# One split instead of two for the weight factors of products 5 and 6 in an output projection

## The chip, the cores and the metric

The kernel runs on one core of one Trainium2 chip. Times are device microseconds (us) of one execution; the time of a kernel is the median of its runs. Engines: PE is TensorE, PEld its weight loads, DVE is VectorE, ACT is ScalarE, POOL is GpSimd, SP is SyncE, which issues the DMAs of the weights.

## The reference

One encoder layer on x of 512 tokens by 1024 channels, all in float32: a feed-forward network, a mixer and a second feed-forward network, each with a norm before and after and a residual.

```python
def swiglu(x, w_in, w_out):
    gate, up = jnp.split(x @ w_in, 2, axis=-1)     # w_in  1024 x 5632
    return (jax.nn.silu(gate) * up) @ w_out        # w_out 2816 x 1024
...
y_mix = mixer(...)      # gated convolution on half of the channels, chunked mLSTM on the other half
```

The change touches only the product with `w_out`, which is done once in each of the two feed-forward networks (FFN).

## The kernel before

**Split numbers.** Each float32 operand of a matmul is split into a high part, rounded to the type that PE multiplies, and a low part, the rest. `split(hi, lo, src)` is two instructions: an ACT copy into `hi` (L273, CAST in the trace) and a DVE subtraction `lo = src - hi` (L274). A product takes three matmuls: hi x hi, hi x lo, lo x hi. So each weight costs a cast on ACT and a subtraction on DVE before PE can use both of its parts.

**The FFN.** The hidden size of 2816 is 22 columns `h` of 128 (`hcol(k)`). The in-projection makes each of them by a scheme of seven products (matmuls at L400, 12 in each product; helpers on DVE L464 to L470 and L448, on ACT L456 to L467). The last column's products are not needed until late in the out-projection, and the scheduler may put them between the out-projection's matmuls.

**The out-projection.** 22 steps over k. The first ten are taken in pairs: a pair of h columns times the two weight rows that belong to it, by seven products instead of eight, with sums and differences of halves as factors. It is done in two passes, by a list `OUT`:

- five "a" steps (pairs 0 to 4): `w_out_a` builds the weight factors of products 1, 7, 5 and 6 from the raw rows r0 (128 x 1024) and the right half of r1 (three subtractions at L183, then splits); `left_a` the factors from h (L492 on DVE, splits into `big`). Matmuls at L525.
- then `taken(1)`, `taken(5)` and so on copy the sums out of PSUM (ACT L535 for product 1, L537 for product 5);
- then five "b" steps (products 2, 3 and 4, `w_out_b`) in turn with plain steps (L550), and the other plain steps.

In the first pass one more number is kept for the second one: the difference that is the sixth factor, `kept` (five tiles of 128 x 512), which `w_out_b` subtracts (L206).

**What sets the order.** The program is written without engine order: the tile scheduler simulates the program and fixes the order of instructions on each engine when it is built. Each engine then runs its queue in that order and waits at the head of it. A change of one instruction's size or engine can therefore move others. Buffers come from pools: 4 raw weight tiles (`rawp`), 12 split weights (`wpool`), 13 of h and its factors (`big`), 6 temporaries of 128 x 512 (`t2`), 2 of 128 x 1024 (`t4`), 8 PSUM banks.

Of the kernel before, what the change touches and what calls it, by code (L numbers as in the profile page):

```python
# [37 lines left out]
def encoder_kernel(ctx: ExitStack, tc: tile.TileContext, a: dict, out: bass.AP):  # L38
    nc = tc.nc
# [14 lines left out]
    def nm(s):  # L54
        uid[0] += 1
        return f"{s}_{uid[0]}"
# [7 lines left out]
    def t2(dt=F32):  # L64
        return t2p.tile([P, 512], dt, tag="t2", name=nm("t2"))
# [7 lines left out]
    def f32(ap):  # L73
        return ap.bitcast(F32)
# [101 lines left out]
    kept = []  # L176

    def w_out_a(r0, r1):

        c = (slice(0, 512), slice(512, 1024))  # L180

        def sub(o, a_, b_):
            nc.vector.tensor_tensor(out=o, in0=a_, in1=b_, op=ALU.subtract)  # L183

        def wt(n):
            return wpool.tile([P, 1024], F32R, tag="w", name=nm(n))

        sub(r1[:, c[0]], r0[:, c[1]], r0[:, c[0]])
        sub(r0[:, c[1]], r1[:, c[1]], r0[:, c[1]])
        t = t2()  # L190
        sub(t, r1[:, c[1]], r1[:, c[0]])
        kept.append(t)
        ah, al = wt("whi"), wt("wlo")
        split(ah, al, r0)
        bh, bl = wt("whi"), wt("wlo")
        split(bh[:, c[0]], bl[:, c[0]], r1[:, c[0]])
        split(bh[:, c[1]], bl[:, c[1]], t)
        return {1: (ah[:, c[0]], al[:, c[0]]), 7: (ah[:, c[1]], al[:, c[1]]),
                5: (bh[:, c[0]], bl[:, c[0]]), 6: (bh[:, c[1]], bl[:, c[1]])}

# [71 lines left out]
    def split(hi, lo, src, eng=nc.vector):  # L272
        nc.scalar.copy(out=hi, in_=src)  # L273
        eng.tensor_tensor(out=lo, in0=src, in1=f32(hi), op=ALU.subtract)  # L274
# [831 lines left out]
```

## Time and profile before

| what | value |
| --- | --- |
| median of 3 runs | 925.3 us (924.71 to 926.23) |
| the profiled execution | 924.99 us, of which the span is 923.3 us |
| granted PE clock | 0.998 |
| PE busy | 906.5 us, 6015 matmuls |
| DVE busy | 713.2 us, 1192 instructions |
| ACT busy | 446.4 us, 753 instructions |
| POOL busy | 42.3 us, 64 instructions |

The span is the profiled time from the first to the last instruction. In rows of a group, "x199 | 240.7, 1217" reads as 199 instructions, 240.7 us in all, 1217 ns each; what follows is the idle time ahead of them and what ended it. In a timeline a row begins with start and duration; equal instructions that follow each other are joined (x12), and brackets give idle time ahead of them and its releaser. In the first FFN the first pass stands at about 232 to 265 us of the span, in the second at about 792 to 825 us.

### The profile page before, as it was taken

What the parts mean: (1) busy time and instruction counts of PE and PEld (TensorE: products, weight loads), DVE (VectorE), ACT (ScalarE), POOL (GpSimd) and SP (SyncE); (2) the same over time, 40 slices, a digit from 0 to 9 for tenths busy, and PEclk for the clock granted to TensorE, in tenths of its full rate; (3) what the DMA queues carried; (4) which work ended last, traced back from release to release, by engine and by line L of the source; (5) the groups of instructions that cost most, each with busy time, mean ns of one, the idle gap of its engine ahead of it and who ended that gap; (6) DMA issues with size and microseconds to landing.
All of it is one profiled execution on the core that took longest, in us unless ns stands there. A gap on an engine that the chain in (4) does not pass through costs nothing.

```text
span 923.3 us, 15016 instructions
## 1 busy us (share of the span) xinstructions
PE 906.5 (98%) x6015; PEld 822.4 (89%) x6015; DVE 713.2 (77%) x1192; ACT 446.4 (48%) x753; POOL 42.3 (5%) x64
## 2 busy tenths in 40 slices
PE   7999999999999999999999999999999999999997
PEld 7999999999877888987888888999999999977885
DVE  5988988888988358496777736889888888999434
ACT  6645555555456226452424425645545544565311
POOL 3000000000012001000011000000000000000000
PEclk9999999999999999999999999999999999999999
DMA  8433434343344514231422501314343333343502
GB/s 246 146 92 92 138 105 125 92 117 95 100 136 139 180 46 115 61 100 46 117 90 69 160 23 30 104 51 137 92 129 101 109 104 97 106 149 100 172 4 88
DMA packets 126542, 96.99 MB, mean 105 GB/s; under 512 B 4212, under 2 KB 114824, under 8 KB 126472
## 3 DMA queue, kind: packets, MB, share of 16 engines
q1 hardware_dynamic: 126472, 96.03, 35.2%
q8 instruction: 47, 0.77, 0.3%
q14 instruction: 23, 0.19, 0.1%
HBM read 93.92 MB, written 2.10 MB: 104 GB/s over the span
## 4 chain that ended last, share of the span: by engine, by line
PE 89%; DVE 6%; ACT 1%; DMA 1%; issue 1%; SPq 0%; POOL 0%; DVEq 0%; POOLq 0%; ACTq 0%
PE ps L400 42%; PE ps L550 13%; PE ps L391 12%; PE ps L525 8%; PE ps L1063 5%; PE ps L421 4%; PE ps L913 2%; DVE big L274 2%; DVE wlo L274 2%; DVE big L492 1%; DMA raw<-in_w_ffn_in_dram 1%; PE ps L980 1%; PE ps L987 1%; PE ps L318 1%; ACT whi L273 0%
## 5 line engine op out<-in xcount | busy, mean ns | idle before, releaser
L274 DVE TENSOR_TENSOR wlo<-raw,whi 128x1024 fp32r<-128x1024 f32 x209 | 247.3, 1192 | 63.7 <-ACT whi L273 47.1
L273 ACT CAST whi<-raw 128x1024 fp32r<-128x1024 f32 x211 | 211.9, 1029 | 153.0 <-DVE raw L150 46.8
L400 PE MATMUL ps<-big,whi 128*128 128x256 f32 x1920 | 264.9, 280 | 0.0
L400 PEld LDWEIGHTS ps<-big,whi 128*128 128x128 f32 x1920 | 243.4, 188 | 0.9 <-ACT whi L273 0.2
L400 PE MATMUL ps<-big,wlo 128*128 128x256 f32 x960 | 150.9, 280 | 0.0
L400 PEld LDWEIGHTS ps<-big,wlo 128*128 128x128 f32 x960 | 129.2, 188 | 0.0
L550 PE MATMUL ps<-whi,big 128*128 128x512 f32 x384 | 122.3, 396 | 0.2 <-ACT whi L273 0.2
L550 PEld LDWEIGHTS ps<-whi,big 128*128 128x128 f32 x384 | 72.0, 188 | 17.7 <-ACT whi L273 0.7
L391 PE MATMUL ps<-big,whi 128*128 128x512 f32 (+1 forms) x384 | 79.8, 358 | 0.0
L525 PE MATMUL ps<-whi,big 128*128 128x512 f32 x240 | 76.1, 395 | 2.8 <-ACT big L273 2.6
L550 PE MATMUL ps<-wlo,big 128*128 128x512 f32 x192 | 75.6, 395 | 0.0
L391 PEld LDWEIGHTS ps<-big,whi 128*128 128x128 f32 x384 | 63.5, 188 | 10.8 <-issue 0.2
L400 PE MATMUL ps<-big,ws 128*128 128x256 f32 x480 | 65.3, 280 | 0.0
L400 PEld LDWEIGHTS ps<-big,ws 128*128 128x128 f32 x480 | 60.3, 188 | 0.0
L525 PEld LDWEIGHTS ps<-whi,big 128*128 128x128 f32 x240 | 44.7, 188 | 13.8 <-ACT big L273 3.5
L462 ACT COPY t<-ps 128x256 f32<-128x256 f32 x40 | 14.9, 372 | 71.4 <-PE ps L400 71.3
L273 ACT CAST big<-big 128x512 fp32r<-128x512 f32 (+2 forms) x68 | 36.1, 583 | 22.7 <-DVE big L492 11.2
L525 PE MATMUL ps<-wlo,big 128*128 128x512 f32 x120 | 44.8, 393 | 0.0
L550 PEld LDWEIGHTS ps<-wlo,big 128*128 128x128 f32 x192 | 36.1, 188 | 8.5
L391 PE MATMUL ps<-big,wlo 128*128 128x512 f32 (+1 forms) x192 | 41.1, 356 | 0.0
L274 DVE TENSOR_TENSOR big<-big,big 128x512 fp32r<-128x512 f32 (+2 forms) x68 | 40.7, 635 | 0.1
L391 PEld LDWEIGHTS ps<-big,wlo 128*128 128x128 f32 x192 | 32.1, 188 | 5.5
(207 smaller groups left out, 1149.6 us busy)
## 6 DMA issues: line engine op xcount, KB each, us to landing
raw<-in_w_ffn_in_dram SPq DMA_DIRECT2D x88, 512.0 KB, 4.8
raw<-in_w_ffn_out_dram SPq DMA_DIRECT2D x44, 512.0 KB, 4.3
raw<-in_w_mix_in_dram SPq DMA_DIRECT2D x24, 512.0 KB, 3.7
raw<-in_w_mix_out_dram SPq DMA_DIRECT2D x8, 512.0 KB, 3.4
raw<-in_w_ffn_out_dram SPq DMA_DIRECT2D x10, 256.0 KB, 4.2
out_dram<-x SPq DMA_DIRECT2D x8, 256.0 KB, 2.9
x<-in_x_dram SPq DMA_DIRECT2D x4, 256.0 KB, 4.5
x<-in_x_dram SPq DMA_DIRECT2D x2, 512.0 KB
```

Source lines behind the costliest of these rows:

```text
L273: nc.scalar.copy(out=hi, in_=src)
L274: eng.tensor_tensor(out=lo, in0=src, in1=f32(hi), op=ALU.subtract)
L318: nc.tensor.transpose(out=pt[:, blk(k)], in_=xs[:, blk(4 * b + k)], identity=ident)
L391: nc.tensor.matmul(o, ww[:, k, :], xk(xT, xx, k, sl), start=n == 0, stop=n == 3 * KD - 1)
L400: nc.tensor.matmul(o, ww[:, k, :], x[xx][:, k, :], start=first and n == 0, stop=n == 11, skip_group_check=True)
L421: nc.tensor.matmul(o, ww[:, k, :], xq_hl(xq, (k // 4, th))[xx][:, k % 4, :], start=n == 0, stop=n == 3 * KD - 1)
L462: nc.scalar.copy(a_[:, h1], x[:, h0])
L492: nc.vector.tensor_tensor(out=o, in0=a_, in1=b_, op=op)
L525: nc.tensor.matmul(acc[tb + t][half], left[n][x][:, blk(t)], right[n][y], start=first and x == y == 0, stop=last_ and x == 1, skip_group_c ...
L550: nc.tensor.matmul(acc[tb][half], hT[hh][:, blk(tb)], w[ww][:, blk(half, 512)], start=fresh and hh == ww == 0, stop=k == NF - 1 and hh == ...
L913: nc.tensor.matmul(pv_, xk(xT, xx, k, blk(tb)), ww[:, k % 2, :], start=n == 0, stop=n == 3 * KD - 1)
L1063: nc.tensor.matmul(acc[half], yy[yi][:, k % 4, blk(tb)], wmo[k][wi][:, blk(half, 512)], start=(n == 0 and yi == 0 and wi == 0), stop=(n == ...
```

## The change

`w_out_a` no longer makes the sixth factor in a tile of its own. The third subtraction writes in place into the right half of r1. The fifth and sixth factor then lie side by side in r1 and are split in one operation of 128 x 1024, instead of two of 128 x 512. An ACT copy of the right half into a `t2` tile keeps the number that `w_out_b` needs.

```diff
         sub(r1[:, c[0]], r0[:, c[1]], r0[:, c[0]])
         sub(r0[:, c[1]], r1[:, c[1]], r0[:, c[1]])
-        t = t2()
-        sub(t, r1[:, c[1]], r1[:, c[0]])
-        kept.append(t)
+        sub(r1[:, c[1]], r1[:, c[1]], r1[:, c[0]])
         ah, al = wt("whi"), wt("wlo")
         split(ah, al, r0)
         bh, bl = wt("whi"), wt("wlo")
-        split(bh[:, c[0]], bl[:, c[0]], r1[:, c[0]])
-        split(bh[:, c[1]], bl[:, c[1]], t)
+        split(bh, bl, r1)
+        t = t2()
+        nc.scalar.copy(t, r1[:, c[1]])
+        kept.append(t)
```

The scheduler's order changes in the two first passes and near them, on PE, DVE and ACT; on POOL and SP it stays. In the rows below a number behind a name tells one buffer's use from another's; it is counted differently in the two programs. `raw` is a loaded weight, `whi` and `wlo` its high and low part, `ps` a PSUM bank, `big` an h tile or the split factors made of it.

PE, start of the first pass in the second FFN, before: `whi_1234` and `whi_1236` are the weights of step 0 (products 1 and 7, and 5 and 6), `whi_1241` those of step 1; the L400 rows are the last hidden column.

```order
L525 MATMUL ps_1251_8663<-whi_1234_8523,big_1261_8673 128x512
L525 MATMUL ps_1252_8664<-whi_1234_8523,big_1261_8673 128x512
L400 MATMUL ps_1245_8551<-big_922_6103,whi_1221_8408 128x256 x8
L400 MATMUL ps_1245_8551<-big_922_6103,wlo_1222_8409 128x256 x4
L525 MATMUL ps_1253_8665<-whi_1236_8527,big_1261_8673 128x512
L525 MATMUL ps_1254_8666<-whi_1236_8527,big_1261_8673 128x512
L400 MATMUL ps_1246_8552<-big_870_5860,whi_1221_8408 128x256 x8
L400 MATMUL ps_1246_8552<-big_870_5860,wlo_1222_8409 128x256 x4
L400 MATMUL ps_1245_8551<-big_923_6106,whi_1223_8412 128x256 x8
L400 MATMUL ps_1245_8551<-big_923_6106,wlo_1224_8413 128x256 x4
L525 MATMUL ps_1251_8663<-whi_1241_8541,big_1263_8708 128x512
L525 MATMUL ps_1252_8664<-whi_1241_8541,big_1263_8708 128x512
```

Before, three products of the last hidden column stand ahead of the first matmul of step 1. After, `whi_1235` holds products 5 and 6 of step 0, `whi_1240` and `whi_1242` the weights of step 1:

```order
L525 MATMUL ps_1251_8656<-whi_1240_8534,big_1263_8701 128x512
L525 MATMUL ps_1252_8657<-whi_1240_8534,big_1263_8701 128x512
L525 MATMUL ps_1255_8660<-whi_1235_8521,big_1261_8666 128x512
L525 MATMUL ps_1253_8658<-whi_1242_8538,big_1263_8701 128x512
L525 MATMUL ps_1254_8659<-whi_1242_8538,big_1263_8701 128x512
L525 MATMUL ps_1255_8660<-whi_1242_8538,big_1263_8701 128x512
L525 MATMUL ps_1251_8656<-wlo_1241_8535,big_1263_8701 128x512
L525 MATMUL ps_1251_8656<-whi_1240_8534,big_1263_8701 128x512
L525 MATMUL ps_1252_8657<-wlo_1241_8535,big_1263_8701 128x512
L525 MATMUL ps_1252_8657<-whi_1240_8534,big_1263_8701 128x512
L400 MATMUL ps_1245_8544<-big_922_6098,whi_1221_8403 128x256 x8
L400 MATMUL ps_1245_8544<-big_922_6098,wlo_1222_8404 128x256 x4
```

The products of the last hidden column moved behind these ten matmuls, nine of which belong to step 1.

DVE, same place, before (`wlo_1222` and `wlo_1224` are weights of the last hidden column, `wlo_1235` and `wlo_1237` those of step 0, `raw_1239` of step 1):

```order
L464 TENSOR_TENSOR t2_1230_8421<-ps_1226_8417,t2_1228_8419 128x256
L183 TENSOR_TENSOR t2_1233_8521<-raw_1232_8517 128x512
L274 TENSOR_TENSOR wlo_1222_8409<-raw_1215_8392,whi_1221_8408 128x1024
L274 TENSOR_TENSOR wlo_1224_8413<-raw_1216_8394,whi_1223_8412 128x1024
L469 TENSOR_TENSOR t2_1229_8420<-ps_1225_8416,t2_1229_8420 128x256
L274 TENSOR_TENSOR wlo_1235_8524<-raw_1231_8515,whi_1234_8523 128x1024
L470 TENSOR_TENSOR big_890_5906<-t2_1229_8420,t2_1230_8421 128x256
L274 TENSOR_TENSOR wlo_1237_8528<-raw_1232_8517,whi_1236_8527 128x512
L274 TENSOR_TENSOR wlo_1237_8528<-t2_1233_8521,whi_1236_8527 128x512
L183 TENSOR_TENSOR raw_1239_8535<-raw_1238_8533 128x512
```

After (`wlo_1234` and `wlo_1236` are step 0's):

```order
L469 TENSOR_TENSOR t2_1229_8415<-ps_1225_8411,t2_1229_8415 128x256
L274 TENSOR_TENSOR wlo_1224_8408<-raw_1216_8389,whi_1223_8407 128x1024
L470 TENSOR_TENSOR big_890_5901<-t2_1229_8415,t2_1230_8416 128x256
L274 TENSOR_TENSOR wlo_1234_8518<-raw_1231_8510,whi_1233_8517 128x1024
L274 TENSOR_TENSOR big_1261_8666<-big_885_5896,big_1261_8666 128x256
L274 TENSOR_TENSOR big_1261_8666<-t4_1262_8667,big_1261_8666 128x256
L183 TENSOR_TENSOR raw_1239_8529<-raw_1238_8527 128x512
L274 TENSOR_TENSOR big_1263_8701<-big_885_5896,big_1263_8701 128x256
L274 TENSOR_TENSOR big_1263_8701<-t4_1264_8702,big_1263_8701 128x256
L492 TENSOR_TENSOR big_885_5896<-t4_1262_8667,big_885_5896 128x256
L448 TENSOR_TENSOR big_890_5901<-ps_1225_8411,t2_1230_8416 128x256
L274 TENSOR_TENSOR wlo_1236_8522<-raw_1232_8512,whi_1235_8521 128x1024
```

L469 moved ahead of a weight's low part, and step 0's second weight moved behind the left factors' low parts and L492, L448.

ACT, end of the a steps in the first FFN, before (`wt_450` and `whi_453` are weights of the next steps, `big_451` the next left factor):

```order
L535 COPY big_414_3035<-ps_406_3027 128x512
L535 COPY big_414_3035<-ps_407_3028 128x512
L537 COPY big_414_3035<-ps_408_3029 128x512
L537 COPY big_414_3035<-ps_409_3030 128x512
L273 CAST wt_450_3246<-raw_447_3242 128x512
L273 CAST whi_453_3294<-raw_452_3292 128x1024
L273 CAST big_451_3286<-big_28_229 128x512
```

After:

```order
L535 COPY big_414_3033<-ps_406_3025 128x512
L273 CAST wt_450_3241<-raw_447_3237 128x512
L273 CAST whi_453_3289<-raw_452_3287 128x1024
L535 COPY big_414_3033<-ps_407_3026 128x512
L537 COPY big_414_3033<-ps_408_3027 128x512
L273 CAST whi_456_3295<-raw_455_3293 128x1024
L537 COPY big_414_3033<-ps_409_3028 128x512
L273 CAST big_451_3281<-big_28_229 128x512
```

Three casts of weights moved between the four copies of the sums.

## The prediction

> **What bounds the kernel now.** I read the busy times first, then what TensorE (PE) waits for, then the busy times of single stretches, and last the timelines around the places where the order changes.
>
> ```profile
> span 923.3 us, 15016 instructions
> ...
> PE 906.5 (98%) x6015; PEld 822.4 (89%) x6015; DVE 713.2 (77%) x1192; ACT 446.4 (48%) x753; POOL 42.3 (5%) x64
> ```
>
> PE is busy in 98% of the span, so only 17 us of idle time exist, and most of them lie elsewhere (start, mixer, end). The waits of PE name those of the output projections' first passes (source line, who released it, total, count, mean, in us):
>
> ```profile
> PE ps L525 <- ACT big L273: 2.6, 2, 1.3
> ...
> PE ps L525 <- ACT wt L273: 0.9, 1, 0.9
> ```
>
> The timeline shows each of them as a gap between rows (start, duration, engine, line). Matmuls of 512 columns follow each other every 0.23 us, so what exceeds 0.23 between two starts is a stall.
>
> ```profile
> 264.66 1.08 PE L525 MATMUL ps<-whi,big 128*128 128x512 f32 x4
> 267.05 0.50 PE L525 MATMUL ps<-whi,big 128*128 128x512 f32 x1 [1.31 <-ACT big L273]
> ...
> 279.76 2.05 PE L525 MATMUL ps<-wt,big 128*128 128x512 f32 x6
> ...
> 809.82 0.39 PE L525 MATMUL ps<-whi,big 128*128 128x512 f32 x1
> 810.40 0.50 PE L525 MATMUL ps<-whi,big 128*128 128x512 f32 x1 [0.19 <-DVE big L448]
> ...
> 839.52 0.39 PE L525 MATMUL ps<-whi,big 128*128 128x512 f32 x1
> 840.81 0.73 PE L525 MATMUL ps<-wt,big 128*128 128x512 f32 x2 [0.90 <-ACT wt L273]
> 841.75 0.50 PE L550 MATMUL ps<-whi,big 128*128 128x512 f32 x1 [0.21 <-ACT whi L273]
> ```
>
> Four matmuls from 264.66 end their starts at 265.35; the next begins at 267.05, so 1.5 us are lost there, and the second wait of 1.3 us in the first list is its twin in the second FFN. The six from 279.76 should take 5 x 0.23 + 0.39 = 1.54 and took 2.05: a stall of some 0.3 inside, the rest being the slower restart. At 810.40 the loss is 0.58 - 0.23 = 0.35; at 840.81 it is 1.29 - 0.23 = 1.06, and up to 841.75 another 0.4. All that the two first passes could give back is therefore about 5 us.
>
> VectorE (DVE) has no such slack where the first pass starts (columns: window, its length, then sum and count for PE, PEld, DVE, ACT and POOL, clock, DMA share, GB/s):
>
> ```profile
> 792.00:800.00 8.00, 8.00 (x55) 7.34 (x54) 7.88 (x18) 4.12 (x9) 0.00 (x0) 1.00 0.30 112
> 800.00:826.00 26.00, 25.71 (x117) 20.59 (x115) 24.96 (x48) 13.32 (x23) 0.00 (x0) 1.00 0.45 142
> ```
>
> DVE is busy 7.88 of 8.00 and 24.96 of 26.00, and still PE loses almost nothing there: DVE is just in time. ScalarE (ACT) is half idle.
>
> **The change, by instructions.** Ten weight steps change, five in each pass.
>
> ```profile
> L274 DVE TENSOR_TENSOR wlo<-raw,whi 128x1024 fp32r<-128x1024 f32 x199 | 240.7, 1217 | 63.7 <-ACT whi L273 47.1 <-PE ps L550 8.8 <-PE ps L525 3.8
> ...
> L274 DVE TENSOR_TENSOR wlo<-t,whi 128x512 fp32r<-128x512 f32 x10 | 6.8, 678 | 0.0
> ...
> L273 ACT CAST whi<-raw 128x1024 fp32r<-128x1024 f32 x201 | 206.2, 1050 | 152.1 <-DVE raw L150 46.8 <-PE ps L391 40.4 <-PE ps L550 34.8
> ...
> L273 ACT CAST whi<-t 128x512 fp32r<-128x512 f32 x10 | 6.2, 619 | 0.0
> ...
> L775 ACT COPY big<-big 4x512 f32<-4x512 f32 x2 | 1.2, 624 | 2.3 <-DVE gm L752 2.3
> ```
>
> DVE: two subtractions of 512 at 0.678 become one of 1024 at 1.217, so 0.14 less by durations; by starts (0.61 and 1.13 apart, below) 0.09. Ten steps: 0.9 to 1.4 us less work. The third subtraction keeps its size and only writes in place. ACT: two casts of 0.619 become one of 1.050, 0.19 less, and a copy of 512 comes on top; no copy of 128 x 512 from SBUF to SBUF in f32 is in the trace, the nearest rows are the 0.619 cast of the same tile and a 0.624 copy, so I take 0.62, and 0.43 more per step, 4.3 in all. Its bounds are -0.19 x 10 = -1.9 (if it all fell into idle time and were free) and +4.3, and ACT's idle 12.7 of 26.00 us in the window above hides it, unless a copy stands directly ahead of a cast for which PE waits; then it costs its 0.5 to 0.6 there. POOL and the DMA queue on SP keep their order; a weight's buffer is now free only after the copy too, up to 0.62 later. That can cost 0 to 0.6 per load; I take 0, since in the walk below DVE reaches each loaded weight after it has landed.
>
> These sums move no time by themselves, since PE is the bound. What moves time is when the first and the second half come out, and where the changed order lets PE meet them.
>
> **The change, by the start of the second FFN's first pass.** Before, these rows stand on DVE, PE and ACT:
>
> ```profile
> 785.53 0.42 DVE L464 TENSOR_TENSOR t<-ps,t 128x256 f32<-128x256 f32 x1 [1.53 <-PE ps L400]
> 785.87 0.68 DVE L183 TENSOR_TENSOR t<-raw 128x512 f32<-128x512 f32 x1
> 786.47 2.35 DVE L274 TENSOR_TENSOR wlo<-raw,whi 128x1024 fp32r<-128x1024 f32 x2
> 788.74 0.41 DVE L469 TENSOR_TENSOR t<-ps,t 128x256 f32<-128x256 f32 x1
> ...
> 791.15 0.68 DVE L274 TENSOR_TENSOR wlo<-t,whi 128x512 fp32r<-128x512 f32 x1
> ...
> 794.74 0.68 DVE L183 TENSOR_TENSOR raw<-raw,raw 128x512 f32<-128x512 f32 x1
> 795.35 0.68 DVE L183 TENSOR_TENSOR t<-raw 128x512 f32<-128x512 f32 x1
> ```
>
> ```profile
> 787.61 0.63 PE L400 MATMUL ps<-big,wlo 128*128 128x256 f32 x4
> ...
> 791.99 0.62 PE L525 MATMUL ps<-whi,big 128*128 128x512 f32 x2
> ...
> 794.26 1.11 PE L400 MATMUL ps<-big,whi 128*128 128x256 f32 x8
> 795.21 0.63 PE L400 MATMUL ps<-big,wlo 128*128 128x256 f32 x4
> ...
> 796.14 1.11 PE L400 MATMUL ps<-big,whi 128*128 128x256 f32 x8
> ...
> 798.51 0.64 PE L400 MATMUL ps<-big,wlo 128*128 128x256 f32 x4
> 798.98 0.86 PE L525 MATMUL ps<-whi,big 128*128 128x512 f32 x3
> ```
>
> ```profile
> 796.45 1.06 ACT L273 CAST whi<-raw 128x1024 fp32r<-128x1024 f32 x1
> ...
> 798.44 0.62 ACT L273 CAST whi<-t 128x512 fp32r<-128x512 f32 x1
> ```
>
> Before, the last hidden column's products (L400, twelve matmuls each, 794.26 to 795.7 and 796.14 to 798.98: three times 1.42, 4.3 us) are sown between the first pass's matmuls, and that is the work that PE does while DVE prepares step 1. In the changed order they stand behind the first nine matmuls of step 1. I walk the changed queues with the durations of these rows; small operations of 256 columns start 0.33 apart (785.53 to 785.87), subtractions of 512 0.61 apart.
>
> DVE. The in-place subtraction now stands ahead of L464 and falls into its 1.53 us of waiting. The weight subtraction after L464 then runs from 785.87 to 787.00. Next in the queue is now L469, which needs the product that PE ends at 787.61 + 0.63 = 788.24: DVE waits 1.3 us, a wait that is new, and the full queue stands behind it. The second weight subtraction goes from 788.67 (before about 787.6), then L470, step 0's first weight from 790.13 to 791.26. Step 0's merged weight stands behind four small subtractions, a subtraction of 512, L492 and L448 (2.6 us): 793.87 to 795.00, where before both halves were done at 791.83. The first subtraction for step 1 that sets product 1's weight moves from 794.74 to 795.33, and the last one, for products 5 and 6, from 795.35 to 797.8.
>
> PE starts the pass at 791.99 as before. Its waits: 0.54 for the cast of the left factor behind L492 (793.7 + 0.6, PE there at 793.8); 0.57 for the merged low weight at 795.00; 0.87 for step 1's first weight (its subtraction ends 795.93, cast 1.05 and the place behind another cast: 797.1, before 797.51); 1.78 for step 1's merged weight (subtraction to 798.4, cast 1.05, 799.6; before its second half came at 799.06). In all 3.8 us, in which before PE did the 4.3 us of L400, less two matmuls (0.46) that the new order has already done. The 25.71 of 26.00 show that nothing later can make it up. If only the merging costs, the loss has the lower end 0.43 (one cast of 1024 instead of a half, 1.050 - 0.619); with all L400 uncovered the upper end is 4.3. I take 3.8, since the order of PE is fixed and its rows lie nearest to that.
>
> The 0.35 at 810.40 goes, as the later L400 leaves L448 long done: -0.35. At 840.81 the casts of wt and of the next weight now stand ahead of eight casts of later left factors: -1.06 - 0.4 = -1.4. The stall of 1.3 before the b steps stays: there the copies of the sums alternate with the weights' casts now, but product 1's sums are closed some 3 us before the end, and the walk gives 1.42 in place of 1.45. Pass 2: 3.8 - 0.35 - 1.4 = **+2.0**.
>
> **The first FFN's pass** goes likewise but keeps its L400 cover (two of three blocks stand early).
>
> ```profile
> 235.70 0.62 ACT L273 CAST whi<-raw 128x512 fp32r<-128x512 f32 x1
> ...
> 263.94 1.08 ACT L537 COPY big<-ps 128x512 f32<-128x512 f32 x2 [1.22 <-PE ps L525]
> 264.90 0.63 ACT L273 CAST wt<-raw 128x512 fp32r<-128x512 f32 x1
> 265.43 1.06 ACT L273 CAST whi<-raw 128x1024 fp32r<-128x1024 f32 x1
> 266.37 4.67 ACT L273 CAST big<-big 128x512 fp32r<-128x512 f32 x10
> ```
>
> The start loses what the merged cast is longer than the half at 235.70, 0.43: +0.4. The 0.3 at 279.76 goes, the weight being done 3 us earlier: -0.3. Before the b steps ACT's rows give PE's restart: 266.37 plus a cast is 267.05. In the changed order three casts (0.53 + 0.95 + 0.95 apart) stand between the four copies (0.54 apart), and product 1's second sum is copied third: counted from the sum that closes 3.2 us before the last, ACT reaches the left factor's cast 0.5 later than now: +0.5. Pass 1: **+0.6** (bounds -0.3 and +1.4).
>
> Sum: 2.0 + 0.6 = +2.6, of which I take 2.5 for DVE's 0.1 per step that shortens the waits. On the profiled execution: 924.99 + 2.5 = 927.5; that run lies 0.3 under the median of 925.3, so 927.8.
>
> The trace's saturated row (24.96 of 26.00) is where the Trainium skill, "Perfetto Trace Analysis", section Optimizing Scalar/DVE Operations, says that grouping into larger operations can improve throughput, if the engine is saturated; by this DVE's 1.4 us would come off, and the median would be 923.9, about rival 1 below. The same section says that where ScalarE and VectorE are not saturated but make others wait, breaking up may let work finish sooner, which speaks against the merge. No run here yet shows which of the two holds.
>
> **The rivals.** A difference of 0.2%, 1.85 us, is about what can be told from none: under 923.45 is faster, over 927.15 slower.
>
> 1. Faster: throughput decides. PE reaches step 1's weights after they are ready, so none of the 3.8 and 0.4 appear, and the removed stalls stay removed: -0.35 - 1.4 - 0.3 and some 0.1 for each of four restarts (0.50 for a first matmul against 0.39), with the tail unchanged: 925.3 - 2.4 = 922.9. It decides if L469 does not hold DVE, which needs its product before 787.0; PE's row ends at 788.24, which speaks against it. Chance 0.12.
> 2. No change: the new waits come to about half, since DVE's order leaves step 1's last subtraction earlier than 797.8 by a microsecond or two: 1.9 in place of 3.8, 925.9 (924 to 927). For it: before, 7.88 of 8.00 busy DVE time cost PE nothing. Against: the subtraction stands behind four operations that before came after it. Chance 0.26.
> 3. A larger loss: the new copies also stand ahead of casts that PE awaits, as one does at the end of pass 2's a steps. Three or four times 0.5, 1.5 to 2 more: 929.6. Against it: ACT's 13.32 of 26.00. Chance 0.12.
>
> That the merge does not happen at all is excluded by the instruction order, which has ten fewer on DVE.
>
> **How the numbers follow.** The forecast has 0.50, with a range of its own from 927.0 to 928.8. Slower: 0.12 and nearly all of 0.50, and a little of rival 2, 0.59. Same: most of rival 2, some of the forecast's edge and of rival 1, 0.31. Faster: rival 1 less its upper edge, 0.10. The range runs from 923.9 (leaves out most of rival 1) to 929.9.
>
> **What would show it.** Right: PE rows of L525 between 792 and 800 with four gaps of 0.5 to 1.8, released by casts and by the merged low weight; L400 blocks only after 799; DVE waiting at L469 about 787; no wait for wt at about 840; 1.05 casts and ten copies of 0.62. Wrong: L400 blocks still ahead of 799 with no gaps before them, DVE reaching step 1's last subtraction before 796.5, or gaps in the rest of the pass, where I have none.

## The result and the profile after

The changed kernel takes **928.33 us** (median of 5 runs, 928.09 to 929.93) against 925.3 (median of 5, 924.6 to 926.23): a ratio of 1.0038, interval 1.0023 to 1.0053. It is slower, as forecast (927.8). The profiled execution took 928.33 us, span 926.6.

The page's busy times after:

```profile
span 926.6 us, 15012 instructions
...
PE 907.1 (98%) x6015; PEld 823.9 (89%) x6015; DVE 713.1 (77%) x1182; ACT 451.8 (49%) x753; POOL 44.6 (5%) x64
```

DVE runs ten instructions fewer and is busy as long as before; ACT is busy 5.4 us longer; PE is busy as long and the span is 3.3 us longer. What PE waits for, in the list of waits:

```profile
PE ps L525 <- ACT big L273: 3.4, 3, 1.8
PE ps L525 <- ACT whi L273: 2.2, 2, 1.5
...
PE ps L525 <- DVE wlo L274: 0.3, 1, 0.3
```

The wait for `wt` is gone, and waits for step weights (`whi`, `wlo`) are new. They stand where the second FFN's first pass starts, in PE's timeline:

```profile
793.28 1.07 PE L525 MATMUL ps<-whi,big 128*128 128x512 f32 x4
794.67 0.49 PE L525 MATMUL ps<-whi,big 128*128 128x512 f32 x1 [0.33 <-ACT big L273]
795.49 0.50 PE L525 MATMUL ps<-wlo,big 128*128 128x512 f32 x1 [0.32 <-DVE wlo L274]
...
796.52 0.40 PE L525 MATMUL ps<-wlo,big 128*128 128x512 f32 x1
797.55 0.96 PE L525 MATMUL ps<-whi,big 128*128 128x512 f32 x3 [0.63 <-ACT whi L273]
800.03 1.65 PE L525 MATMUL ps<-whi,big 128*128 128x512 f32 x3 [1.53 <-ACT whi L273]
801.48 0.63 PE L525 MATMUL ps<-wlo,big 128*128 128x512 f32 x1
...
802.76 0.63 PE L525 MATMUL ps<-whi,big 128*128 128x512 f32 x1
803.19 1.17 PE L400 MATMUL ps<-big,whi 128*128 128x256 f32 x8
```

Four gaps, and only then the last hidden column's products (L400), which before filled this stretch. Counted as starts beyond the normal 0.23, the gaps are 0.48, 0.58, 0.79 and 1.69, in all 3.5 us. Behind the last one something else is to be seen: matmuls last 0.63 instead of 0.39 and start 0.43 apart. Seven of them, from 800.03 to 803.19, took 3.16 instead of 7 x 0.23 = 1.61: another **1.55 us**. The windows give the reason (the column before the DMA share is the granted clock):

```profile
800.00:802.00 2.00, 1.97 (x5) 1.58 (x6) 2.00 (x4) 1.04 (x3) 0.00 (x0) 0.50 0.39 33
802.00:804.00 2.00, 2.00 (x11) 1.71 (x10) 2.00 (x5) 0.00 (x0) 0.00 (x0) 0.67 0.57 229
```

Before, both of these stretches had a clock of 1.00.

On DVE and ACT the same place reads:

```profile
785.91 0.42 DVE L464 TENSOR_TENSOR t<-ps,t 128x256 f32<-128x256 f32 x1 [0.93 <-PE ps L400]
...
788.66 0.42 DVE L469 TENSOR_TENSOR t<-ps,t 128x256 f32<-128x256 f32 x1 [1.19 <-PE ps L400]
...
794.22 1.21 DVE L274 TENSOR_TENSOR wlo<-raw,whi 128x1024 fp32r<-128x1024 f32 x1
...
797.57 1.28 DVE L183 TENSOR_TENSOR raw<-raw 128x512 f32<-128x512 f32 x2
```

```profile
794.00 0.62 ACT L273 CAST big<-big 128x512 fp32r<-128x512 f32 x1 [2.31 <-DVE big L492]
796.45 1.04 ACT L273 CAST whi<-raw 128x1024 fp32r<-128x1024 f32 x1 [1.83 <-DVE raw L183]
...
798.93 1.04 ACT L273 CAST whi<-raw 128x1024 fp32r<-128x1024 f32 x1 [0.61 <-DVE raw L183]
799.89 0.61 ACT L196 COPY t<-raw 128x512 f32<-128x512 f32 x1
800.41 0.36 ACT L456 COPY t<-ps 128x256 f32<-128x256 f32 x1
```

DVE waits 1.19 at L469 and reaches step 1's last subtraction at about 798.2. ACT stands idle for 2.31 and 1.83 us, while L456, the copy of the last hidden column's first sum, whose matmuls ended by about 791, waits at 800.41 behind step 1's casts and behind the new copy (L196). Before, it ran nine microseconds earlier:

```profile
791.08 0.37 ACT L456 COPY t<-ps 128x256 f32<-128x256 f32 x1
```

Until L456 has copied the first sum, the column's next product that adds to the same PSUM bank cannot start; that is why its products could not fill PE's gaps.

For the runs below, one profiled execution of each is cut in two by PE rows: A goes from the first of PE's transposes (about 10 us) to the first transpose after the first FFN (346 us), B from there to the end of the last matmul. So the loads ahead of the transposes, which vary, are left out. A still holds some variation that the change does not make. At the matmul that starts at 220 us in the kernel before, ahead of the first changed instruction on any engine, the others have already lost between -0.2 and 1.3 us within A (changed 0.3, nocopy 0.6, nocopy_half 0.2, merge_pool 1.3). Differences in A of up to about 1 us therefore say little. Every profile also has half clock in its first 16 us and behind the last matmul; the last column leaves these out.

| kernel | median (range) | A | B | half clock seen |
| --- | --- | --- | --- | --- |
| before | 925.3 (924.6 to 926.23) | 336.1 | 571.1 | no |
| changed | 928.33 (928.09 to 929.93) | 336.6 | 574.0 | in B, 1.55 us |

### The profile page after: what moved, and what is told of

It reads as the page before. It is cut to its first block, busy times and chain, and to the rows that moved or that the text cites. A ratio compares the mean times of both kernels' runs of the same rounds, so it can differ in the third digit from the quotient of the medians.

```text
span 926.6 us, 15012 instructions
## 1 busy us (share of the span) xinstructions
PE 907.1 (98%) x6015; PEld 823.9 (89%) x6015; DVE 713.1 (77%) x1182; ACT 451.8 (49%) x753; POOL 44.6 (5%) x64
## 4 chain that ended last, share of the span: by engine, by line
PE 94%; DVE 3%; ACT 1%; issue 1%; DMA 1%; SPq 0%; POOL 0%; DVEq 0%; POOLq 0%; ACTq 0%
PE ps L400 42%; PE ps L550 14%; PE ps L391 12%; PE ps L525 10%; PE ps L1063 5%; PE ps L421 4%; PE ps L913 2%; DVE wlo L274 1%; PE ps L318 1%; PE ps L980 1%; PE ps L987 1%; DMA gb<-in_norm_ffn_pre_dram 1%; ACT whi L273 1%; PE ps L949 0%; DVE big L274 0%
## 5 line engine op out<-in xcount | busy, mean ns | idle before, releaser
L274 DVE TENSOR_TENSOR wlo<-raw,whi 128x1024 fp32r<-128x1024 f32 x209 | 253.0, 1218 | 67.2 <-ACT whi L273 49.9
L273 ACT CAST whi<-raw 128x1024 fp32r<-128x1024 f32 x211 | 216.7, 1049 | 157.2 <-DVE raw L150 45.7
L400 PE MATMUL ps<-big,whi 128*128 128x256 f32 x1920 | 264.5, 280 | 0.0
L400 PEld LDWEIGHTS ps<-big,whi 128*128 128x128 f32 x1920 | 243.4, 188 | 0.6
L400 PE MATMUL ps<-big,wlo 128*128 128x256 f32 x960 | 150.7, 280 | 0.0
L400 PEld LDWEIGHTS ps<-big,wlo 128*128 128x128 f32 x960 | 129.1, 188 | 0.0
L550 PE MATMUL ps<-whi,big 128*128 128x512 f32 x384 | 122.6, 395 | 0.0
L525 PE MATMUL ps<-whi,big 128*128 128x512 f32 x240 | 79.5, 401 | 5.5 <-ACT big L273 3.4
L550 PE MATMUL ps<-wlo,big 128*128 128x512 f32 x192 | 75.8, 395 | 0.0
L400 PE MATMUL ps<-big,ws 128*128 128x256 f32 x480 | 65.2, 280 | 0.0
L400 PEld LDWEIGHTS ps<-big,ws 128*128 128x128 f32 x480 | 60.2, 188 | 0.0
L525 PE MATMUL ps<-wlo,big 128*128 128x512 f32 x120 | 47.6, 398 | 0.3 <-DVE wlo L274 0.3
```

The lines of the kernel that those rows point to most:

```text
L400: nc.tensor.matmul(o, ww[:, k, :], x[xx][:, k, :], start=first and n == 0, stop=n == 11, skip_group_check=True)
L525: nc.tensor.matmul(acc[tb + t][half], left[n][x][:, blk(t)], right[n][y], start=first and x == y == 0, stop=last_ and x == 1, skip_group_c ...
L550: nc.tensor.matmul(acc[tb][half], hT[hh][:, blk(tb)], w[ww][:, blk(half, 512)], start=fresh and hh == ww == 0, stop=k == NF - 1 and hh == ...
```

## The experiments

Each was timed beside the kernel before, whose median in the three sets was 925.36, 925.3 and 925.13.

| kernel | median (range) | ratio to before (interval) | A | B | half clock seen |
| --- | --- | --- | --- | --- | --- |
| half_keep | 927.83 (926.31 to 929.73) | 1.0027 (1.0019 to 1.0036) | 337.2 | 572.3 | no |
| nocopy | 927.51 (925.69 to 928.88) | 1.0022 (1.0013 to 1.0031) | 337.9 | 572.4 | in A and B |
| nocopy_half | 927.02 (924.55 to 930.13) | 1.0017 (1.0007 to 1.0027) | 338.0 | 572.5 | in A and B |
| defer | 924.74 (923.36 to 927.02) | 0.9999 (0.9989 to 1.0008) | 335.6 | 570.9 | no |
| merge_pool | 926.22 (925.53 to 928.88) | 1.0017 (1.0008 to 1.0026) | 337.7 | 571.7 | no |
| fill12 | 927.85 (926.83 to 929.78) | 1.0031 (1.002 to 1.0041) | 338.5 | 572.5 | in A |
| after_left | 924.71 (923.58 to 926.12) | 0.9996 (0.9987 to 1.0004) | 335.0 | 571.5 | no |
| after_left_fill | 924.06 (923.14 to 924.58) | 0.9989 (0.998 to 0.9997) | 334.1 | 571.5 | no |
| defer_left | 922.04 (921.63 to 924.95) | 0.9971 (0.996 to 0.9982) | 334.7 | 569.8 | no |
| **early_left** | **920.78** (920.29 to 921.21) | 0.9952 (0.994 to 0.9964) | 334.6 | 568.3 | no |

The theory after the result: not the merged split costs time but the copy that keeps the sixth factor. It fills a temporary that stands in the program ahead of the last hidden column's own temporaries, and the scheduler then puts that column's copies and products behind step 1. The kernel before takes this temporary at nearly the same place in the program, but there DVE's subtraction fills it, and L456 ran at 791.08, ahead of the one for step 1 at 795.35. So it is not enough that the temporary is taken first; what is new is the copy that fills it. The rival is what the prediction had walked through as one thing: the halves come out later because they are merged.

**half_keep**: the merge undone, the copy kept.

```diff
-        split(bh, bl, r1)
+        split(bh[:, c[0]], bl[:, c[0]], r1[:, c[0]])
+        split(bh[:, c[1]], bl[:, c[1]], r1[:, c[1]])
```

> The in-place subtraction and the ACT copy stay, but products 5 and 6 are split in two operations of 512 again. If the merge is what cost time (the second half comes too late), this is back at 925.3, within 1. If it is the copy, traced ahead of the last hidden column's own copies on ACT, which pushes that column's products (L400) behind step 1, the loss stays: 927 to 929, with PE waits of about 1.9, 0.6 and 0.3 for step 1's casts and 0.6 at L400 in the first 10 us of the second FFN's first pass (a walk of this order with the durations of before).

It stays slow, 927.83. PE's timeline:

```profile
797.79 0.98 PE L526 MATMUL ps<-whi,big 128*128 128x512 f32 x3 [1.56 <-ACT whi L274]
799.14 1.16 PE L526 MATMUL ps<-whi,big 128*128 128x512 f32 x3 [0.37 <-ACT whi L274]
800.59 1.21 PE L401 MATMUL ps<-big,whi 128*128 128x256 f32 x8 [0.29 <-ACT t L457]
```

Waits for step 1's casts, and the first product of the last hidden column directly waits for ACT's copy (L457 here, L456 before). With two splits of 512 the loss stays, so the merge is not needed for it.

**nocopy** and **nocopy_half**: no copy is made, and the b steps subtract another number of the same size; with the merged split and with two splits.

```diff
-        t = t2()
-        nc.scalar.copy(t, r1[:, c[1]])
-        kept.append(t)
...
-        nc.vector.tensor_tensor(out=r1[:, c[0]], in0=r1[:, c[0]], in1=kept.pop(0), op=ALU.subtract)
+        nc.vector.tensor_tensor(out=r1[:, c[0]], in0=r1[:, c[0]], in1=r1[:, c[1]], op=ALU.subtract)
```

> Merged split as changed, but no copy is made; the b steps subtract the right half of their own raw row instead of the kept number, so product 4 has another factor, at the same cost. If the merge costs: 928 still, with the four waits at the start of the second FFN's first pass. If the copy's place does: none of these waits, the last hidden column's products ahead of step 1 as before, and by the walk some 926.5, since waits of about 1.1 and 1.0 for casts come later in that pass and the one before the b steps grows from 1.5 to 2.4.

> As nocopy (no copy is made, product 4 takes another factor), but with products 5 and 6 split in two operations of 512. Against nocopy it gives the price of the merge with no copy in the program. Merge harmless: equal to nocopy within 1 us once stretches at a granted clock of 0.5 are set apart; merge harmful: 2 us or more faster than nocopy; merge useful by freed DVE time: 1 us or more slower.

None of the waits at the pass's start is left in nocopy: PE goes from the last hidden column straight into the first pass and back,

```profile
797.49 0.62 PE L522 MATMUL ps<-whi,big 128*128 128x512 f32 x2
797.95 1.11 PE L397 MATMUL ps<-big,whi 128*128 128x256 f32 x8
798.89 0.63 PE L397 MATMUL ps<-big,wlo 128*128 128x256 f32 x4
799.36 0.40 PE L522 MATMUL ps<-wlo,big 128*128 128x512 f32 x1
```

but the time, 927.51, was higher than the 926.5 expected. The starts ahead of the b steps lie 2.2 us apart, against 1.7 in the kernel before, and behind them the clock fell, in both FFNs:

```profile
266.52 0.40 PE L522 MATMUL ps<-whi,big 128*128 128x512 f32 x1
268.72 0.50 PE L522 MATMUL ps<-whi,big 128*128 128x512 f32 x1 [1.81 <-ACT big L270]
...
270.04 0.63 PE L522 MATMUL ps<-whi,big 128*128 128x512 f32 x1
```

nocopy_half gives the price of the merge by itself. Its median is 0.5 us lower (927.02 against 927.51), and each median lies inside the other's range. Both profiles have the half clock twice, and A + B is 910.4 in each; counted from 220 us on, so without the start, nocopy's execution is about 0.3 us the shorter one. The two measures point opposite ways: the merge alone **cannot be told from 0**, and by the intervals of the two ratios it is worth no more than about 1 us either way.

The wait ahead of the first FFN's b steps is another matter. Its starts lie 1.71 us apart in the kernel before, 2.19 in the changed one, 2.20 in half_keep and nocopy, 2.62 in nocopy_half, which has neither merge nor copy, and 1.62 in defer below. So neither the merge nor the copy is needed for this growth, and what it hangs on stays open. With the half clock behind it, it is a main reason why the two kernels without a copy are still slower than the kernel before.

**defer**: merged split and ACT copy, but the copy is written where the a step is consumed.

```diff
-        t = t2()
-        nc.scalar.copy(t, r1[:, c[1]])
-        kept.append(t)
+        owed.append(r1[:, c[1]])
...
                 left, right = left_a(n), w_get(1)
+                t = t2()
+                nc.scalar.copy(t, owed.pop(0))
+                kept.append(t)
```

> Merged split and ACT copy as changed, but the copy is written in the program where the step is consumed, not where its weights are split, so it stands behind the last hidden column's copies. Copy's place decides: no waits in the first 8 us of the second FFN's first pass, 926.5 to 927 with waits of about 1.1 and 1.0 at its fourth step and 2.4 before the b steps. Merge decides: 928 or more, with the waits for step 0's merged low part and step 1's casts in place.

The same work as the changed kernel, and the loss is gone: 924.74, ratio 0.9999. The last hidden column's first copy (L454 here, L456 before) stands ahead of step 1's casts again, and its products cover PE again:

```profile
786.09 0.36 ACT L454 COPY t<-ps 128x256 f32<-128x256 f32 x1
```

```profile
795.30 1.11 PE L398 MATMUL ps<-big,whi 128*128 128x256 f32 x8
...
796.95 0.85 PE L523 MATMUL ps<-whi,big 128*128 128x512 f32 x3
```

It was faster than expected. The waits at the fourth step and the 2.0 before the second FFN's b steps came. What makes up for them, in PE's rows beside those of the kernel before, are the stalls that are gone near 280 (0.6 us) and near 840 (1.6 us); they are gone in the changed kernel too. The waits at the fourth step:

```profile
814.75 1.20 PE L523 MATMUL ps<-whi,big 128*128 128x512 f32 x4 [0.67 <-ACT whi L271]
816.54 1.20 PE L523 MATMUL ps<-whi,big 128*128 128x512 f32 x4 [0.60 <-ACT whi L271]
```

So 3.6 us of the medians hang on where in the program the copy and its temporary are written, with merge and copy both in place. The two ranges do not overlap.

**merge_pool**: the changed kernel with the copy on POOL (`nc.gpsimd.tensor_copy` in place of `nc.scalar.copy`).

> The changed kernel with the kept number copied by POOL instead of ACT. If the copy's place in ACT's queue pushes the last hidden column's copies back, POOL frees them: no waits for step 1's casts, 925.5. If it is the tile itself (taken from the six temporaries in the program ahead of the last hidden column's own three), these copies and their products stay behind step 1's casts: waits of about 1.5 and 1.0 in the second FFN, 1.4 before its b steps, 927 (by the walk 0.9 to 1.2 less than the changed kernel).

926.22 lies halfway between the two expectations, but the waits are those of the second: 1.4 and 0.9 us for step 1's casts and 1.6 before the second FFN's b steps. Taking the copy out of ACT's queue doesn't bring the cover back. ACT's timeline says why:

```profile
795.51 1.04 ACT L273 CAST whi<-raw 128x1024 fp32r<-128x1024 f32 x1 [3.87 <-DVE raw L183]
...
797.51 1.04 ACT L273 CAST whi<-raw 128x1024 fp32r<-128x1024 f32 x1
798.45 0.36 ACT L456 COPY t<-ps 128x256 f32<-128x256 f32 x1
```

ACT idles 3.87 us with L456 ready but placed behind step 1's two casts. It is the order, not ACT's load. Which rule of the scheduler makes it so stays open; its inside was not looked at. The runs point to the temporary together with the copy that fills it late, on whichever engine, but no run moves the one without the other.

**fill12**: twelve matmuls of zeros in the longest new gap of the changed kernel; on PE, DVE and ACT nothing else moves.

```diff
...
+                    for _ in range(warm_up if t == 1 and x == y == 0 else 0):
+                        fed["warm"] = nc.tensor.matmul(
+                            acc[tb + t][half][:, 0:256], warm[:, 0:P], warm, start=False, stop=False, skip_group_check=True)
...
```

> The changed kernel with twelve matmuls of zeros (128 x 256, bf16) added to a sum, in the longest of the new gaps (1.7 us ahead of step 1's merged weight in the second FFN); no other instruction moves. If the granted clock of 0.50 at 800 to 802 and 0.67 at 802 to 804 us comes of PE idling in the stretch ahead of it, the clock stays at 1.00 there and the time falls by about 1.5 to 926.8. If the clock falls for another cause, it stays 928.3 or rises by up to 1 (twelve matmuls at half rate outlast the gap).

In the profile the stretch behaves as expected, and B is 1.5 shorter than the changed kernel's:

```profile
798.85 1.48 PE L539 MATMUL ps<-warm 128*128 128x256 bf16 x12
...
800.76 0.97 PE L534 MATMUL ps<-whi,big 128*128 128x512 f32 x3 [0.20 <-ACT whi L273]
```

But in this execution the clock fell at another place, behind the starts that lie 2.19 us apart ahead of the first FFN's b steps, where the changed kernel's profile has no fall, and the median is only 0.5 lower, with overlapping ranges. As a timing it is inconclusive. The profile settles little either, since after_left below keeps its full clock behind an unfilled gap at the same place.

**early_left** and **after_left**, **defer_left**: in the kernel before, the changed one and defer, the left factors of the first b step are written earlier (n == SEVEN - 1 in after_left).

```diff
+        lefts = {}
...
+                if n == SEVEN - 2:
+                    for b in range(1):
+                        lefts[b] = left_b(b)
                 for m in (1, 5, 6, 7):
...
-                left, right = left_b(n), w_get(2)
+                left, right = lefts.pop(n) if n in lefts else left_b(n), w_get(2)
```

> The kernel before, with the left factors of the first b step (two ACT casts and the DVE work) written in the program ahead of the fourth a step's products instead of behind the sums' copies. If the waits of 1.5 us ahead of each first b step come of these casts standing behind the four copies of the sums on ACT, both go, and with them those at 280 and 840: by the walk 3 to 4 us less, 921.5. If the copies themselves are late (they read sums that PE closes last), the waits stay and the time is 925.3.

> The changed kernel, with the first b step's left factors written ahead of the last a step's products. The waits of 2.0 and 1.4 us before the b steps should go, those at the start of the second FFN's first pass stay, the stretch at half clock behind them with them in most runs: some 3.5 less than the changed kernel, 924.8. If the waits only move, 928.

> Merged split, the copy written where the step is consumed, and the first b step's left factors written ahead of the fourth a step's products. If the merge with its copy out of the way costs nothing, this lies by 2.5 to 3.5 under the kernel before, near early_left: 922. If the freed DVE time (0.9 us in ten steps) counts at all, it is the faster of the two; if the longer held weight buffers count, the slower.

All three times came as expected (920.78, 924.71, 922.04). after_left's expectation counted on half clock in most runs, though, and its profiled execution (924.65) has none, so part of that agreement is luck. In early_left the list of waits has nothing left of the first passes but one of 0.5:

```profile
PE ps L525 <- DVE big L448: 0.5, 1, 0.5
```

early_left is the **fastest version**, 4.5 us under the kernel before. With the same edit on both, the merged version with its copy deferred is 1.3 us slower: merge and copy together bring nothing here even at their best, and the weights come 1.1 and 0.8 us late at the fourth step (starts at 812.61 and 814.78, followed by gaps of 1.37 and 1.00, less 0.23).

**after_left_fill**: after_left with fill12's matmuls; the only long gap left is filled.

> The kernel after_left (whose runs went from 923.6 to 926.1, median 924.7) with the twelve matmuls of zeros in the gap ahead of step 1's merged weight. If idle PE time makes the clock fall in some of its executions, the upper ones go and the median with them, to 924.2 or less and a range under 1.5. If not, median and range stay, and the fall at 800 us in the changed kernel had another cause.

Median 924.06, range 1.44 us wide; after_left's was 2.54 wide, at 924.71. Both moved as expected for a clock that falls in some executions. But the two were timed in different sets, on two chips, and the intervals of the two ratios overlap, so neither the effect nor its size (0.65) is settled. after_left's own profile has the gap and no fall:

```profile
799.13 0.97 PE L525 MATMUL ps<-whi,big 128*128 128x512 f32 x3 [1.51 <-ACT whi L273]
799.94 0.40 PE L525 MATMUL ps<-wlo,big 128*128 128x512 f32 x1
```

## Why the prediction was right, and where it wasn't

- **The start of pass 2**: predicted waits 0.54, 0.57, 0.87, 1.78; measured 0.48, 0.58, 0.79, 1.69 (3.5 instead of 3.8). DVE's new wait at L469 was put at 1.3 and was 1.19; step 1's last subtraction was put at 797.8 and began at about 798.2. L400 stood behind, as the order said.
- **What was missed**: the 1.55 us at half clock behind these waits. No term stood for it; before, no gap of 1.7 us or less had such a stretch behind it.
- **Pass 2's other terms**: the 0.35 at 810 and the 1.4 at 840 are gone. The wait before the b steps was put at 1.42: 832.41 - 830.79 - 0.23 = 1.39.

```profile
830.79 0.40 PE L525 MATMUL ps<-whi,big 128*128 128x512 f32 x1
832.41 0.50 PE L525 MATMUL ps<-whi,big 128*128 128x512 f32 x1 [1.23 <-ACT big L273]
...
844.97 0.39 PE L525 MATMUL ps<-wt,big 128*128 128x512 f32 x1
```

- **Pass 1**: +0.6 was predicted. The b-step wait grew by 0.49 (268.02 - 265.83 = 2.19 against 1.70), predicted 0.5; the stall at 280 is gone, and with its two slow restarts it was worth 0.6, not 0.3; the start lost 0.2 instead of 0.4. A rose by 0.5, of which 0.3 lies ahead of the pass. This term was too large by some 0.4.

```profile
265.83 0.39 PE L525 MATMUL ps<-whi,big 128*128 128x512 f32 x1
268.02 0.50 PE L525 MATMUL ps<-whi,big 128*128 128x512 f32 x1 [1.80 <-ACT big L273]
```

- **DVE and ACT**: the ten copies took 0.616 each (predicted 0.62). The merged and single low parts together take 253.0 instead of 240.7 + 6.8 + 6.8, 1.3 us less (predicted 0.9 to 1.4), and no run shows that any of it came off the time.

```profile
L274 DVE TENSOR_TENSOR wlo<-raw,whi 128x1024 fp32r<-128x1024 f32 x209 | 253.0, 1218 | 67.2 <-ACT whi L273 49.9 <-PE ps L550 9.5 <-PE ps L525 3.8
```

So the sum (2.5) came near the measured 3.0 (3.3 in the profiled executions, of which 0.3 lies ahead of the changed code) by luck in part, because errors cancelled. The 1.55 at half clock was left out. Against it stood 0.5 too much in the starts of the two passes, 0.3 too little for the stall at 280, and 0.4 that the second FFN recovered beyond the terms counted (3.54 + 1.55 - 0.35 - 1.4 = 3.3, while B rose by 2.9).

The mechanism was right in its second half. The prediction says: "What moves time is when the first and the second half come out, and where the changed order lets PE meet them." The order did move the time, with the waits, their places and their releasers as walked. That the merged halves themselves move it is not borne out: half_keep has the loss without merged halves, defer and nocopy have merged halves without the waits at the start of the pass. What moved the order there is the copy, whose cost the prediction took to be hidden by ACT's idle time; with the copy written later in the program, these waits and the loss are gone (defer).

Rival 1 (throughput decides) is not borne out by nocopy against nocopy_half, where less DVE work gave no gain that can be told. Of the two statements drawn from the Trainium skill ("Perfetto Trace Analysis", section Optimizing Scalar/DVE Operations), neither shows here: grouping on an engine at 24.96 of 26.00 gave no gain that can be told, and breaking up again (half_keep, 927.83 against 928.33, with overlapping ranges) gave none either. Rival 3's mechanism, a copy ahead of casts that PE awaits, exists at 799.89, but what it delays is L456, not a cast.

## What to carry to other kernels

Where a scheduler orders the queues, an added operation with a buffer of its own is not priced by its duration: look what stands behind it in the order, and which work had been covering PE there. If a change loses, try writing the new operation later in the program before giving up the change; here that alone was worth 3.6 us. And read the waits that were there before the change: the left factors whose two casts stood behind four copies were worth 4.5 us, more than the whole change.

## What the runs showed of the hardware

- **After a gap of about 2 us PE may run at half clock.** Starts 1.9 us or more apart in a first pass or ahead of the b steps occur twelve times in the profiles of these kernels, one execution of each. After six of them matmuls ran at half rate (clock 0.50) for some 3 us, for about 1.5 us more; after the other six (half_keep's 2.20 and 2.00, defer's 2.25 among them) the clock stayed at 1.00. After the gaps up to 1.85 us in these stretches it never fell. The spread of the runs fits: nocopy_half with gaps of 2.5 us went from 924.55 to 930.13 in 12 runs, early_left without such gaps from 920.29 to 921.21 in 5. That the gap makes the clock fall is not settled, since fill12 and after_left_fill are inconclusive. The Trainium skill, "TensorE: Matmul & The Clock Gate", section Part 1, tells of a free-running window of activity, so that a change of clock depends on where in the window the work falls; six falls in twelve agree with that. The same section puts half clock behind at least one idle window of about 3.4 us, and here 1.9 to 2.6 us sufficed.
- **A POOL copy of 128 x 512 may take many times its shortest time.** In merge_pool the ten copies took from 0.61 to 6.04 us (least, median and most, in ns, in the first row below). The shortest of the second FFN ran while DVE waited, the longest while DVE was busy throughout (the window's sums are PE, PEld, DVE 2.00 of 2.00, ACT and POOL). No run sets the cause apart. On ACT the same copies took 0.61 to 0.62.

```profile
L196 POOL COPY t<-raw x10: 612/1174/6037, 223.4 to 820.6; 128x512 f32<-128x512 f32 x10
```

```profile
785.21 0.61 POOL L196 COPY t<-raw 128x512 f32<-128x512 f32 x1 [201.54 <-DVE raw L183]
797.44 6.79 POOL L196 COPY t<-raw 128x512 f32<-128x512 f32 x2 [11.62 <-DVE raw L183]
```

```profile
798.00:800.00 2.00, 1.40 (x9) 1.31 (x10) 2.00 (x4) 1.39 (x4) 2.00 (x1) 1.00 0.00 0
```
